# A four-head conv and retention trunk in fp32: Strassen over all 16 K tiles, sample dot products on ScalarE, and pairs that overlap

## The chip, the core and the metric

One core of one Trainium2 chip runs the whole program. The metric is the device time of one execution in microseconds; the median over runs is compared. The kernel has five engines to spread its work over: TensorE (PE in the profile, its weight loads PEld), VectorE (DVE), ScalarE (ACT), GpSimd (POOL) and SyncE (SP), which here only issues DMAs.

## The reference

Two layers (DEPTH = 2) of a hybrid decoder are run for a prompt of 512 positions and for 8 samples of one new position each; the kernel treats them as one matrix of T = 520 columns. Everything is fp32. The core of one layer:

```python
h = rmsnorm(x, norm_g)
z = h @ w_in                      # 2048 -> 8192
b_c, c_c, x_c, g_c, q, k, v, g_r = split_projection(z)
conv_y, new_buf = short_conv(c_c * x_c, conv_buf, conv_w)
y_conv = b_c * conv_y * jax.nn.silu(g_c)
q = rope(q.reshape(Bsz, L, RET_HEADS, RET_HEAD_DIM), pos)
k = rope(k.reshape(Bsz, L, RET_HEADS, RET_HEAD_DIM), pos) * (RET_HEAD_DIM ** -0.5)
...
o, new_S = retention(q, k, v, ret_S.astype(jnp.float32), retention_log_gamma())
...
x = x + jnp.concatenate([y_conv, y_ret], axis=-1) @ w_out
x = x + jax.nn.sigmoid(x @ w_pg) * (p_i @ w_ple)
```

Retention has 4 heads of 256. For a sample there is only one position, so a head's step is a rank-one update of its 256 x 256 state with k and v, and then the product of q with the new state: 256 dot products. The states and the last conv inputs are outputs too.

## The kernel before

**Tiles and pairs.** D = 2048 is 16 K tiles of 128. Every big product (w_in, w_out, w_pg) goes by *pairs*: two blocks of 128 output rows, each 520 columns wide in two halves of 260 (LEFT and RIGHT). A product in fp32 is three fp32r matmuls (`mm3`, L247 to L249): weight high part by operand high and low part, weight low part by operand high part. High and low parts of the weights are made on the core by `split_w`: ScalarE copies the rounded high part (L229), VectorE subtracts it for the low part (L230). They lie in a ring of 60 tiles of 128 columns (SPLIT), the raw weights in one of 32 (RAW).

**Strassen.** `pair` computes two output blocks either with `plain` (64 tile products) or with `strassen` over the first s K tiles, in Winograd's form: seven products of s/2 tiles instead of eight, with four sums of weight blocks on VectorE (`add`, L319) and sums of the operands' halves (`operand_sums`, L413 to L416), which are made once and shared by all pairs. The other 16 - s tiles are added in the ordinary way. With s < 16 four PSUM banks hold the sums (a, b, c, d), with s = 16 three do. ScalarE copies banks to slots or to other banks (`copy`), VectorE adds them up (`plus`); both are recorded at L307. Five banks (`Banks`) serve these products.

**Which s a pair has.** The tables HEADS, CONVS, OUT_ROWS and GATES name s for each pair. Before, the pairs of the heads are at 14 (after 0 and 8 at the start of layer 0, 0 at the start of layer 1), and the conv pairs at 14, 14, then 13 times 16, then 14.

**Stages of a layer.** Heads: for each of 4 heads four pairs (q, k, v, gate), `rope` and `silu` on VectorE and ScalarE, and the chunked retention of the prompt in nine steps taken up between pairs (`later`, `aside`). Conv: 16 pairs, with a short convolution on VectorE. Then 8 output pairs and 8 gate pairs (the last pair of the last layer is taken apart).

**Sample steps.** `sample_step` is called between and within pairs of heads and convs, 32 times a layer. It loads one state (`st`, 128 x 512) and one row of q and k on all partitions (`kb`), decays the state on ScalarE (L776), adds k times v on VectorE in two halves (L780), sends the state out from GpSimd's queue (L781), and takes the dot products with q on VectorE, each half with one multiply-and-sum instruction (L784), which the chip runs as the main instruction and a read of the accumulator. `osum` collects them until `sample_norm` at the end of the convs.

**What sets the order.** The code issues instructions in program order with priorities (`tc.high_priority`, with WPRIO for the weights' splits and sums), and a scheduler then orders each engine's queue with a simulated timeline. Each engine runs its queue in order; semaphores join them. SP issues the weight loads.

Of the kernel before, what the change touches and what calls it, by code (L numbers as in the profile page):

```python
# [9 lines left out]
AF = mybir.ActivationFunctionType  # L10
# [3 lines left out]
P = 128  # L14
D = 2048
KT = D // P
DEPTH = 2
SEQ = 512
NS = 8
# [32 lines left out]

HEADS = [[0, 0, 0, 8] + [14] * 12, [0] + [14] * 15]
CONVS = [[14] * 2 + [16] * 13 + [14]] * 2
OUT_ROWS = [[0, 8, 16, 16, 16, 16, 16, 0]] * 2
# [136 lines left out]
def trunk_kernel(  # L192
# [69 lines left out]
    def acc(n):  # L262
        return [banks.get() for _ in range(n)]
# [25 lines left out]

    def strassen(x, src0, src1, s, step=None):  # L290

# [3 lines left out]
        ops = x.ops  # L295
        x.supply(min(s + CH, KT))
        assert len(x.sums) >= q
        k1, k2 = at(ops, range(0, s, 2), LEFT), range(1, s, 2)
        t1, t2, t3, t4 = ([t[i] for t in x.sums[:q]] for i in range(4))
        step = step or (lambda n: None)  # L300
        a, b, d = acc(3)
        c = banks.get() if s < KT else None
        z0, z1 = get(), get()

        def early(fn, *args):
# [29 lines left out]

        w11 = raws(src0, 0)
        times(a, w11, k1, True, False)
        step(1)
        copy(d, a)
        w21, w22 = raws(src1, 0), raws(src1, q)  # L340
# [14 lines left out]
        if c is None:  # L355
            copy(z0[:, LEFT], d)
        aside()
        times(a, w11, t3, False, True)
        raw_ring.put(w11)
        step(5)  # L360
        if c is None:
            plus(z1[:, RIGHT], a, z1[:, RIGHT])
        else:
            copy(z1[:, LEFT], a)
        while middle:
            middle.pop(0)()
        times(b, w21, at(ops, k2, RIGHT), False, True)
        raw_ring.put(w21)
        step(6)
        if c is None:  # L370
            plus(z0[:, RIGHT], b, z0[:, RIGHT])
        times(a, w22, t4, False, True)
# [12 lines left out]
        if c is not None:  # L385
            plus(z1[:, RIGHT], c, z1[:, LEFT])
            copy(z0[:, LEFT], d)
            plus(z0[:, RIGHT], b, z0[:, RIGHT])
            banks.put(c)
        copy(z1[:, LEFT], a)  # L390
        banks.put(d, b, a)
        step(8)
# [3 lines left out]
    def pair(x, src, m, n, nxt=None):  # L396
# [4 lines left out]
        if s:  # L401
            z = strassen(x, src[m], src[m + 1], s, (lambda i: x.free(i, nxt)) if last else None)
        else:
            z = plain(x, src[m], src[m + 1], (lambda a, b: x.free_tiles(a, b, nxt)) if last else None)
# [18 lines left out]
    class Operands:  # L423


        def __init__(self, rows, load, reserve=0, whole=False, gain=None):
            self.rows, self.load, self.reserve, self.whole, self.gain = rows, load, reserve, whole, gain
            self.sent = []
            self.ops = [None] * KT
            self.sums = []  # L430
            self.ready = 0
            first = max(rows[0], min(FIRST, max(rows))) // 2
# [283 lines left out]
    for l in range(DEPTH):  # L716
# [57 lines left out]
        def sample_step(h, b, st, kb):  # L774

            keep(S.activation(st[:, :512], st[:, :512], AF.Identity, scale=gam(h)))  # L776
            k = kb[:, 256:512]
            for e in range(2):
                c = slice(256 * e, 256 * e + 256)
                keep(V.scalar_tensor_tensor(st[:, c], k, vs[:, h, e, b : b + 1], st[:, c], MUL, ADD))  # L780
            SIDE.dma_start(o_rets[l, h, b], st[:, :512])  # L781
            for e in range(2):
                c = slice(256 * e, 256 * e + 256)
                V.tensor_tensor_reduce(k, st[:, c], kb[:, :256], 1.0, 0.0, MUL, ADD, osum[:, e, h, b : b + 1])  # L784
            put(st, kb)
# [31 lines left out]
        def retain(h):  # L817
# [10 lines left out]
            for d in range(2):  # L828
                S.activation(qks[:, d, :NS], q[d][:, SEQ:T], AF.Copy)
            aside_copy(h, 0, q)  # L830
# [6 lines left out]
            for d in range(2):  # L837
                S.activation(qks[:, 2 + d, :NS], kf[d][:, SEQ:T], AF.Copy)
            aside_copy(h, 2, kf)
# [639 lines left out]
```

## Time and profile before

| | |
|---|---|
| median of 3 runs | 2169.55 us (2167.43 to 2171.86) |
| the profiled execution's span | 2167.3 us |
| between its span and the runs' median | 2.25 us |
| PE busy | 2147.8 us, 99%, 17861 matmuls |
| DVE busy | 1896.1 us, 87% |
| ACT busy | 1264.5 us, 58% |
| POOL busy | 430.6 us, 20% |
| DMA | 387.31 MB, mean 179 GB/s |

A row of a group of instructions has the line, the engine, the operation, what is written and read with shapes, the count, then the busy time in us and the mean of one in ns, and last the idle time of the engine just before them and what ended it. A row of waits has who waited for whom, the us in total, how often, and the longest. A row of windows has the stretch, its length, then busy time and count of PE, PEld, DVE, ACT and POOL, the granted clock of TensorE, and the DMA's share and rate. Matmuls overlap each other, so 282 ns for one is its length in the pipeline, and not the distance from one to the next.

### The profile page before, as it was taken

To read this page: it belongs to the slowest core of one execution; us is meant where nothing else is said; L and a number is where in the kernel's file an instruction comes from. 1 tells how busy PE (TensorE), PEld (TensorE's weight loads), DVE (VectorE), ACT (ScalarE), POOL (GpSimd) and SP (SyncE) were. 2 spreads that over 40 slices of the span, in tenths; PEclk is the share of its full clock that TensorE was granted. 3 is DMA by queue.
4 is the path that set the end of the run, shared out by engine and by line. 5 is a ranking of instruction groups with operands and counts; after the bars stand their busy time and mean duration, and the time that the engine had idled before them with its cause. 6 is when DMAs were issued, how large, how long until landed. Compare 5 with 4: busy or idle time off the path is not lost. (4 is left out here: it accounts for less than half of the span.)

```text
span 2167.3 us, 48178 instructions
## 1 busy us (share of the span) xinstructions
PE 2147.8 (99%) x17861; PEld 2142.1 (99%) x17861; DVE 1896.1 (87%) x3849; ACT 1264.5 (58%) x2647; POOL 430.6 (20%) x746
## 2 busy tenths in 40 slices
PE   9999999999999999999999999999999999999998
PEld 9999999999999999999999999999999999999998
DVE  8889988998999987987997988989999998879884
ACT  8656655565555655655765655565645555456565
POOL 2313222211001211200212222231111022011011
PEclk9999999999999999999999999999999999999999
DMA  8555565545543745645645566664464355566455
GB/s 288 171 175 197 181 217 184 178 157 175 158 129 118 238 156 187 215 154 160 215 144 175 172 213 191 189 209 170 151 182 149 120 158 202 176 207 200 128 164 198
DMA packets 182861, 387.31 MB, mean 179 GB/s; under 512 B 25888, under 2 KB 56352, under 8 KB 182624
## 3 DMA queue, kind: packets, MB, share of 16 engines
q1 hardware_dynamic: 128704, 212.98, 31.6%
q0 software_dynamic: 53056, 169.84, 23.8%
q8 instruction: 140, 2.29, 0.4%
q10 hardware_dynamic: 864, 1.39, 0.2%
q14 instruction: 97, 0.79, 0.1%
HBM read 318.96 MB, written 65.15 MB: 177 GB/s over the span
## 5 line engine op out<-in xcount | busy, mean ns | idle before, releaser
L247 PE MATMUL ps_g<-slot,split 128*128 128x260 f32 x5465 | 1531.6, 284 | 7.2 <-ACT slot L307 2.9
L248 PE MATMUL ps_g<-slot,split 128*128 128x260 f32 x5465 | 1534.3, 282 | 0.3 <-DVE slot L555 0.3
L249 PE MATMUL ps_g<-slot,split 128*128 128x260 f32 x5461 | 1519.9, 283 | 0.5 <-DVE split L230 0.5
L229 ACT ACTIVATE split<-raw 128x512 fp32r<-128x512 f32 (+2 forms) x1347 | 777.3, 596 | 583.1 <-DVE raw L319 213.2
L247 PEld LDWEIGHTS ps_g<-slot,split 128*128 128x128 f32 x5465 | 1024.0, 188 | 10.1 <-ACT slot L307 3.7
L248 PEld LDWEIGHTS ps_g<-slot,split 128*128 128x128 f32 x5465 | 1028.5, 188 | 0.5 <-DVE slot L555 0.5
L249 PEld LDWEIGHTS ps_g<-slot,split 128*128 128x128 f32 x5461 | 1019.8, 188 | 1.0 <-DVE split L230 1.0
L230 DVE TENSOR_TENSOR split<-raw,split 128x512 fp32r<-128x512 f32 (+2 forms) x1346 | 849.2, 652 | 172.5 <-PE ps_g L248 85.4
L319 DVE TENSOR_TENSOR raw<-raw 128x512 f32<-128x512 f32 (+1 forms) x660 | 428.9, 660 | 32.5 <-DMA raw<-wi 23.7
L307 ACT ACTIVATE slot<-ps_g 128x260 f32<-128x260 f32 x336 | 127.4, 381 | 140.6 <-PE ps_g L249 122.7
L551 ACT ACTIVATE slot<-slot 128x520 fp32r<-128x520 f32 (+1 forms) x212 | 109.2, 562 | 46.6 <-DVE slot L414 11.1
L552 DVE TENSOR_TENSOR slot<-slot,slot 128x520 fp32r<-128x520 f32 (+1 forms) x212 | 124.4, 620 | 4.1 <-ACT slot L551 3.9
L781 POOL DMA_DIRECT2D o_rets<-slot x64 | 35.3, 552 | 351.6 <-DVE slot L780 131.7
L307 DVE TENSOR_TENSOR slot<-ps_g,slot 128x260 f32<-128x260 f32 x168 | 70.9, 424 | 6.0 <-PE ps_g L249 3.7
L869 POOL DMA_DIRECT2D slot<-hs x64 | 46.2, 724 | 118.7 <-DVE split L230 42.7
L814 POOL DMA_DIRECT2D hs<-slot x64 | 35.6, 556 | 139.3 <-DVE slot L755 61.3
L780 DVE SCALAR_TENSOR_TENSOR slot<-slot,vs,slot 128x256 f32<-128x256 f32 x128 | 56.1, 481 | 4.5 <-ACT slot L776 4.3
L746 DVE TENSOR_TENSOR slot<-slot,slot 128x520 f32<-128x520 f32 x80 | 55.8, 698 | 4.7 <-DMA o_rets<-slot 3.7
L770 POOL DMA_DIRECT2D slot<-sret x64 | 35.5, 554 | 114.6 <-ACT split L229 37.3
L1058 POOL DMA_DIRECT2D slot<-x1s x76 | 40.8, 538 | 87.6 <-PE ps_g L249 27.2
L1209 POOL DMA_DIRECT2D x2s<-slot x30 | 16.4, 545 | 201.6 <-DVE slot L1204 200.6
L771 POOL DMA_DIRECT2D slot<-kq x64 | 34.9, 547 | 106.0 <-DVE slot L876 22.2
(217 smaller groups left out, 1733.8 us busy)
## 6 DMA issues: line engine op xcount, KB each, us to landing
raw<-wi SPq DMA_DIRECT2D x377, 256.0 KB, 3.9
raw<-wo SPq DMA_DIRECT2D x128, 256.0 KB, 5.4
raw<-wg SPq DMA_DIRECT2D x122, 256.0 KB, 4.1
raw<-wi SPq DMA_DIRECT2D x136, 192.0 KB, 4.0
slot<-x1s POOLq DMA_DIRECT2D x76, 260.0 KB, 5.1
slot<-sret POOLq DMA_DIRECT2D x64, 256.0 KB, 4.0
hs<-slot POOLq DMA_DIRECT2D x64, 256.0 KB, 4.0
slot<-hs POOLq DMA_DIRECT2D x64, 256.0 KB, 5.2
```

The costliest lines, as they stand in the source:

```text
L229: S.activation(hi, raw, AF.Copy)
L230: V.tensor_tensor(lo, raw, F(hi), SUB)
L247: PE.matmul(out, wh, xh, start=start, stop=False, skip_group_check=more)
L248: PE.matmul(out, wh, xl, start=False, stop=False, skip_group_check=more)
L249: PE.matmul(out, wl, xh, start=False, stop=stop, skip_group_check=more)
L307: fn(*args)
L319: V.tensor_tensor(out[:, n], x[:, n], y[:, n], op)
L551: keep(S.activation(hi, src[:, n], AF.Copy))
L552: V.tensor_tensor(lo, src[:, n], F(hi), SUB)
L746: V.tensor_tensor(out[:, n], v, table[:, n], MUL)
L780: keep(V.scalar_tensor_tensor(st[:, c], k, vs[:, h, e, b : b + 1], st[:, c], MUL, ADD))
L869: SIDE.dma_start(t[:, :512].rearrange("p (m n) -> p m n", m=2), src)
```

## The change

Four edits.

1. The tables: 12 + 15 head pairs go from 14 to 16 tiles, and the first two conv pairs of each layer too. Only the last conv pair of a layer stays at 14.
2. `strassen` with s = 16 takes its sixth product (b) ahead of the fifth (a), and gives banks back as soon as they are read: d after its copy, b after its sum.
3. If the next pair has 16 tiles as well, the first product of that pair and the copy of it (`begin`) are issued ahead of this pair's last product, and handed over in `x.begun`. This holds for heads, convs, output and gate pairs.
4. `sample_step`: one product on VectorE of the whole state (512 columns) with q, which is read twice by a broadcast; then ScalarE sums each half with an ACTIVATE Copy whose accumulator goes to `osum`. For that, k and q change places in `qks` and `kb`.

```diff
-HEADS = [[0, 0, 0, 8] + [14] * 12, [0] + [14] * 15]
-CONVS = [[14] * 2 + [16] * 13 + [14]] * 2
+HEADS = [[0, 0, 0, 8] + [16] * 12, [0] + [16] * 15]
+CONVS = [[16] * 15 + [14]] * 2
...
-    def strassen(x, src0, src1, s, step=None):
+    def strassen(x, src0, src1, s, step=None, ahead=None):
...
-        a, b, d = acc(3)
-        c = banks.get() if s < KT else None
-        z0, z1 = get(), get()
...
-        w11 = raws(src0, 0)
-        times(a, w11, k1, True, False)
+        def begin(src):
+            a, d = acc(2)
+            w = raws(src, 0)
+            times(a, w, k1, True, False)
+            copy(d, a)
+            return a, d, w
+
+        a, d, w11 = x.begun or begin(src0)
+        x.begun = None
+        b = banks.get()
+        c = None if whole else banks.get()
+        z0, z1 = get(), get()
         step(1)
-        copy(d, a)
...
         if c is None:
             copy(z0[:, LEFT], d)
+            banks.put(d)
         aside()
+        if whole:
+            times(b, w21, at(ops, k2, RIGHT), False, True)
+            raw_ring.put(w21)
+            step(6)
+            plus(z0[:, RIGHT], b, z0[:, RIGHT])
+            banks.put(b)
         times(a, w11, t3, False, True)
...
-        times(b, w21, at(ops, k2, RIGHT), False, True)
-        raw_ring.put(w21)
-        step(6)
-        if c is None:
-            plus(z0[:, RIGHT], b, z0[:, RIGHT])
+        if not whole:
+            times(b, w21, at(ops, k2, RIGHT), False, True)
+            raw_ring.put(w21)
+            step(6)
+        elif ahead is not None and len(banks.free) > 1 and all(ops[0:KT:2]):
+            x.begun = begin(ahead)
         times(a, w22, t4, False, True)
...
-            z = strassen(x, src[m], src[m + 1], s, (lambda i: x.free(i, nxt)) if last else None)
+            z = strassen(x, src[m], src[m + 1], s, (lambda i: x.free(i, nxt)) if last else None,
+                         src[m + 2] if s == KT and x.rows[n + 1 : n + 2] == [KT] else None)
...
-            k = kb[:, 256:512]
+            k, q = kb[:, :256], kb[:, 256:512]
...
+            both = kb[:, :512].rearrange("p (e d) -> p e d", e=2)
+            V.tensor_tensor(both, st[:, :512].rearrange("p (e d) -> p e d", e=2), q.unsqueeze(1).broadcast_to([P, 2, 256]), MUL)
             for e in range(2):
-                c = slice(256 * e, 256 * e + 256)
-                V.tensor_tensor_reduce(k, st[:, c], kb[:, :256], 1.0, 0.0, MUL, ADD, osum[:, e, h, b : b + 1])
+                S.activation(both[:, e], both[:, e], AF.Copy, accum_out=osum[:, e, h, b : b + 1])
```

What the scheduler makes of it is seen in the engines' orders. First, ScalarE where one pair passes into the next in the heads of layer 0, before. `ps_g_3624` is the first bank (a) of the next pair, `ps_g_3626` its d, and `ps_g_3308` the bank a of this pair, whose last eviction is the last row; `split` are weights' high parts, and `ps_o` belongs to the retention.

```order
L229 ACTIVATE split_73<-raw_72 128x512 x2
L307 ACTIVATE ps_g_3626<-ps_g_3624 128x260
L229 ACTIVATE split_73<-raw_72 128x384
L988 ACTIVATE slot10_247_3475<-ps_o_3452,shift_3465,rstp_3464 128x256 x2
...
L229 ACTIVATE split_73<-raw_72 128x512
L307 ACTIVATE slot54_243_3313<-ps_g_3308 128x260
```

The same place with the change, where `ps_g_4691` is the next pair's a, `ps_g_4692` its d, and `ps_g_4387` this pair's a (`ps_kt` is of the retention).

```order
L935 ACTIVATE slot57_302_4616<-ps_kt_4611,vec_74 128x256
L229 ACTIVATE split_73<-raw_72 128x512 x4
L304 ACTIVATE ps_g_4692<-ps_g_4691 128x260
L229 ACTIVATE split_73<-raw_72 128x512
L304 ACTIVATE slot27_298_4490<-ps_g_4387 128x260
```

In both, the copy of the next pair's first product stands ahead of this pair's last eviction; what moved is that now all splits are 512 wide.

Second, a sample step on VectorE in the heads of layer 0, before: `slot65_238_3286` is the state, `slot3_239_3287` holds q and k.

```order
L780 SCALAR_TENSOR_TENSOR slot65_238_3286<-slot3_239_3287,vs_81,slot65_238_3286 128x256 x2
L230 TENSOR_TENSOR split_73<-raw_72,split_73 128x512
L230 TENSOR_TENSOR split_73<-raw_72,split_73 128x384
L230 TENSOR_TENSOR split_73<-raw_72,split_73 128x512
L784 ISA slot3_239_3287,osum_82<-slot65_238_3286,slot3_239_3287 128x256
L784 ISA osum_82 128x1
```

With the change, VectorE at a step of layer 0's heads (`slot61_277_4190` the state, `slot3_278_4191` k and q), and after it ScalarE around the sums of the same step.

```order
L797 SCALAR_TENSOR_TENSOR slot61_277_4190<-slot3_278_4191,vs_81,slot61_277_4190 128x256 x2
L230 TENSOR_TENSOR split_73<-raw_72,split_73 128x512
L800 TENSOR_TENSOR slot3_278_4191<-slot61_277_4190,slot3_278_4191 128x512
L230 TENSOR_TENSOR split_73<-raw_72,split_73 128x512
L304 TENSOR_TENSOR slot60_281_4207<-ps_g_4206,slot60_281_4207 128x260
```

```order
L847 ACTIVATE qks_3908<-slot64_276_3912 128x8
L229 ACTIVATE split_73<-raw_72 128x512 x4
L802 ACTIVATE slot3_278_4191,osum_82<-slot3_278_4191 128x256 x2
L229 ACTIVATE split_73<-raw_72 128x512
L304 ACTIVATE ps_g_4388<-ps_g_4387 128x260
L229 ACTIVATE split_73<-raw_72 128x512
```

The two sums with their reads have left VectorE's queue, one product has come, and the sums now stand in ScalarE's queue among the splits and evictions.

More of the change, by code (lines that the diff above doesn't have):

```diff
@@ L296, in strassen @@
         x.supply(min(s + CH, KT))
+        whole = s == KT
         assert len(x.sums) >= q
@@ L360, in strassen @@
         step(5)
-        if c is None:
+        if whole:
             plus(z1[:, RIGHT], a, z1[:, RIGHT])
@@ L366, in strassen @@
             middle.pop(0)()
-        times(b, w21, at(ops, k2, RIGHT), False, True)
-        raw_ring.put(w21)
-        step(6)
-        if c is None:
-            plus(z0[:, RIGHT], b, z0[:, RIGHT])
+        if not whole:
[4 more added lines that the diff above has]
+            x.begun = begin(ahead)
         times(a, w22, t4, False, True)
@@ L389, in strassen @@
             banks.put(c)
+            banks.put(d, b)
         copy(z1[:, LEFT], a)
-        banks.put(d, b, a)
+        banks.put(a)
         step(8)
@@ L430, in __init__ @@
             self.sums = []
+            self.begun = None
             self.ready = 0
@@ L828, in retain @@
             for d in range(2):
-                S.activation(qks[:, d, :NS], q[d][:, SEQ:T], AF.Copy)
+                S.activation(qks[:, 2 + d, :NS], q[d][:, SEQ:T], AF.Copy)
             aside_copy(h, 0, q)
@@ L837, in retain @@
             for d in range(2):
-                S.activation(qks[:, 2 + d, :NS], kf[d][:, SEQ:T], AF.Copy)
+                S.activation(qks[:, d, :NS], kf[d][:, SEQ:T], AF.Copy)
             aside_copy(h, 2, kf)
```

## The prediction

> **What bounds the kernel now.** I read the page first: busy time of each engine, and the rows over the span for TensorE and its clock.
>
> ```profile
> span 2167.3 us, 48178 instructions
> PE 2147.8 (99%) x17861; PEld 2142.1 (99%) x17861; DVE 1896.1 (87%) x3849; ACT 1264.5 (58%) x2647; POOL 430.6 (20%) x746
> PE   9999999999999999999999999999999999999998
> PEclk9999999999999999999999999999999999999999
> ```
>
> TensorE is busy all the way at the full granted clock. The span is 2167.3 us and the runs' median 2169.55, so 2.25 us lie around the span. I make the sum on the span and add them back.
>
> Next came the waits of TensorE. A busy PE could still be a PE that is fed late, so what it waited for decides.
>
> ```profile
> PE ps_g L247 <- ACT slot L307: 2.9, 4, 1.3
> PE ps_g L247 <- ACT ps_g L307: 1.6, 2, 1.2
> PE ps_g L247 <- ACT split L229: 1.5, 2, 1.3
> PE ps_vt L913 <- DMA slot<-hs: 0.9, 1, 0.9
> PE ps_g L249 <- DVE split L230: 0.5, 1, 0.5
> ```
>
> These are total, times and longest. In 2167 us TensorE lost under 10 us to other engines, 6.0 us of it before a product's first matmul (L247) for an eviction or a split.
>
> Third, the windows, to see where VectorE stands in the stages that the change touches. The first is one plain stretch in the heads; the second answer has the heads of layer 0, its conv pairs of 16 tiles, and the same two stages of layer 1.
>
> ```profile
> 200.00:250.00 50.00, 50.00 (x420) 50.00 (x419) 47.05 (x101) 30.28 (x67) 10.12 (x17) 1.00 0.60 184
> ```
>
> ```profile
> core 0: us, PE busy (x) PEld busy (x) DVE busy (x) ACT busy (x) POOL busy (x), PEclk, DMA share, GB/s
> 101.00:400.00 299.00, 299.00 (x2501) 298.93 (x2500) 269.80 (x600) 179.43 (x397) 79.94 (x139) 1.00 0.60 191
> 424.00:664.00 240.00, 239.06 (x1997) 238.88 (x1996) 221.23 (x436) 134.61 (x272) 29.43 (x50) 1.00 0.49 151
> 1144.00:1464.00 320.00, 319.79 (x2675) 319.50 (x2675) 283.68 (x629) 189.48 (x419) 82.47 (x140) 1.00 0.61 191
> 1488.00:1700.00 212.00, 211.76 (x1768) 211.35 (x1767) 192.67 (x378) 118.54 (x242) 28.95 (x49) 1.00 0.51 158
> ```
>
> In the heads 420 matmuls pass in 50 us, one per 0.119 us, with VectorE at 94% in that stretch and 90.2% over the whole of layer 0's heads. So a matmul taken away is worth 0.119 us as long as VectorE keeps up, and VectorE is the engine to watch.
>
> **The change, part by part.**
>
> *Fewer matmuls.* A pair of s tiles by Strassen has 7 products of s/2 tiles, and the other 16 - s tiles cost 4 tile products each; a tile product is 3 matmuls. At 14 that is 49 + 8 = 57, at 16 it is 56: 3 matmuls less for each pair. The number of pairs: HEADS has 12 + 15 rows that go from 14 to 16, CONVS 2 in each layer, 31 in all (the last conv pair stays at 14). The built order agrees: it has 93 matmuls less. 93 x 0.119 = 11.1 us off TensorE, all on the path that sets the end.
>
> The Trainium skill, "TensorE: Matmul & The Clock Gate", section "Wait — 56ns, not 53.3ns?", puts a warm matmul's start to start at N / 2.4 GHz plus about 2.5 ns. For 260 columns that would be 110.8 ns and 10.3 us, an estimate from that page; this trace has 119 ns, and the measurement decides.
>
> *The weights' work on VectorE and ScalarE.* The rows by shape:
>
> ```profile
> L230 DVE TENSOR_TENSOR split<-raw,split 128x512 fp32r<-128x512 f32 x1031 | 695.0, 690 | 147.8 <-PE ps_g L248 81.2 <-ACT split L229 51.8 <-issue 6.1
> L229 ACT ACTIVATE split<-raw 128x512 fp32r<-128x512 f32 x1032 | 632.3, 626 | 462.3 <-DVE raw L319 188.2 <-PE ps_g L249 166.4 <-PE ps_g L248 45.1
> L319 DVE TENSOR_TENSOR raw<-raw 128x512 f32<-128x512 f32 x520 | 354.1, 688 | 17.6 <-DMA raw<-wi 12.1 <-DMA raw<-wo 2.9
> L230 DVE TENSOR_TENSOR split<-raw,split 128x384 fp32r<-128x384 f32 x249 | 137.1, 555 | 16.2 <-ACT split L229 9.9 <-PE ps_g L248 3.4 <-ACT slot L551 1.9
> L229 ACT ACTIVATE split<-raw 128x384 fp32r<-128x384 f32 x249 | 127.2, 518 | 84.0 <-DVE raw L319 25.0 <-PE ps_g L248 24.2 <-PE ps_g L249 17.9
> L319 DVE TENSOR_TENSOR raw<-raw 128x384 f32<-128x384 f32 x140 | 77.4, 554 | 14.9 <-DMA raw<-wi 11.6 <-DMA raw<-wg 2.8
> L230 DVE TENSOR_TENSOR split<-raw,split 128x256 fp32r<-128x256 f32 x66 | 27.3, 423 | 8.5 <-ACT split L229 7.6 <-PE ps_g L248 0.8
> L229 ACT ACTIVATE split<-raw 128x256 fp32r<-128x256 f32 x66 | 27.3, 415 | 36.7 <-DMA raw<-wi 29.0 <-PE ps_g L248 5.2 <-PE ps_g L249 1.9
> L307 ACT ACTIVATE ps_g<-ps_g 128x260 f32<-128x260 f32 x121 | 45.1, 373 | 16.4 <-PE ps_g L249 16.1
> ```
>
> A pair of 14 splits 7 x (512 + 384) columns and twice 256; a pair of 16 splits 14 x 512. VectorE: 14 x 0.690 = 9.66 us instead of 7 x (0.690 + 0.555) + 2 x 0.423 = 9.56. Its four weight sums: 8 x 0.688 = 5.50 instead of 4 x (0.688 + 0.554) = 4.97. Together +0.635 us a pair, +19.7 us in 31 pairs. ScalarE: splits 8.76 instead of 8.84, and one copy from bank to bank less (0.373): -0.45 us a pair, -13.9 us. SyncE has two weight loads less a pair, of the same bytes. None of this is on the path while TensorE is fed.
>
> *The dot products.* Each of the 64 sample steps had two multiply-and-sum instructions on VectorE, each with a read of the accumulator. Now it has one 512-wide product there and two summing copies on ScalarE.
>
> ```profile
> L784 DVE CUSTOM_DVE_ANT_0 slot<-slot,slot 128x256 f32<-128x256 f32 x128 | 53.9, 421 | 0.0
> L784 DVE DVE_READ_ACCUMULATOR2_ANT osum<- 128x1 f32 x128 | 11.1, 87 | 0.0
> ```
>
> VectorE: 2 x (0.421 + 0.087) = 1.016 goes, one product at the 0.688 of a 512-wide sum comes: -0.328 us a step, -21.0 us in 64. The net on VectorE over the kernel is -1.3 us. ScalarE's summing form does not stand in the trace: I take 0.415, the 256-wide copy, since the work is the same, and 0.415 + 0.087 as the other end if its accumulator is read out as VectorE's is. That is 53 to 64 us, so ScalarE's net is +39 to +50 us on 1264.5, about 61% of the new span. On the path I take 0. What hides it is the lead of the split weights.
>
> ```profile
> ACT split L229 <- PE ps_g L248: 21.9, 32, 2.3
> ACT split L229 <- PE ps_g L249: 18.8, 33, 1.8
> ```
>
> In 101 to 400 us ScalarE stood 65 times until TensorE had freed a piece of the split ring, that is, with the ring full. The new sums wait for VectorE's product, and behind them in ScalarE's queue stand splits and evictions, for which VectorE and TensorE wait; a full ring of 60 tiles, at 8 high and 8 low tiles and 24 matmuls a product, is 3.75 x 24 x 0.119 = 10.7 us of cover. Without any cover 64 x 0.83 = 53 us would show.
>
> The Trainium skill, "ScalarE: Activation LUTs", section "Rules for kernel authors", says to give add and multiply to VectorE, not ScalarE, which speaks against this edit. In this trace the 256-wide copy on ScalarE (0.415) costs no more than the 256-wide product and sum on VectorE (0.421 and 0.087), and ScalarE is the idler engine.
>
> *Pairs run into each other.* The next pair's first product and its copy are now emitted ahead of this pair's last product. But in the order before, ScalarE's copy of the next pair's first product already stood ahead of this pair's last eviction: the scheduler had done this. So I take 0. The ends are -6.0 us (all three L247 waits above go) and +6.0 us (as many new ones). The sum of the last pair of operands in layer 0 is now due at the third pair; it stands 8 splits later in the new order, so its end is 8 x 0.69 = 5.5 us of loss, and I take 0, as it is due only at the end of that pair's second product.
>
> *VectorE in the heads, where the room is least.* Pairs and steps in the windows of layer 0, heads first, then convs:
>
> ```profile
> L319 DVE TENSOR_TENSOR raw<-raw 128x512 f32<-128x512 f32 (+1 forms) x102 | 62.1, 620 | 1.3 <-DMA raw<-wi 0.9
> L784 DVE CUSTOM_DVE_ANT_0 slot<-slot,slot 128x256 f32<-128x256 f32 x39 | 16.4, 422 | 0.0
> ```
>
> ```profile
> L319 DVE TENSOR_TENSOR raw<-raw 128x512 f32<-128x512 f32 x91 | 61.9, 689 | 2.4 <-DMA raw<-wi 2.1
> ```
>
> 102 sums at 8 a pair are 12.75 pairs, and 39 sums are 19.5 steps. VectorE goes from 269.8 to 269.8 + 12.75 x 0.635 - 19.5 x 0.328 = 271.5 us, TensorE from 299 to 299 - 12.75 x 0.357 = 294.4: 92.2%. The conv pairs of 16 now have 221.23 of 240, 92.2% as well, and TensorE was busy 239.06 of them. So the load that the heads get is one that the kernel already carries. Layer 1 has more room (283.68 of 320 now).
>
> The sum: 2167.3 - 11.1 = 2156.2 us of span, plus 2.25 around it: 2158.5 us.
>
> **The rivals.**
>
> *Slower: VectorE's gaps are latency, not room.* In 101 to 400 us VectorE idles 299 - 269.8 = 29.2 us, 2.29 a pair. If it needs all of these, its chain takes 271.5 + 29.2 = 300.7 us against TensorE's 294.4: 0.49 us a pair, 13.3 us in the 27 head pairs, and the gain of 11.1 turns into a loss of 2.2. The sums in ScalarE's queue add to it: VectorE now waits 69.3 us for splits, by these rows,
>
> ```profile
> L229 ACT ACTIVATE split<-raw 128x512 fp32r<-128x512 f32 (+2 forms) x1347 | 777.3, 596 | 583.1 <-DVE raw L319 213.2 <-PE ps_g L249 186.2 <-DMA raw<-wi 75.6
> L230 DVE TENSOR_TENSOR split<-raw,split 128x512 fp32r<-128x512 f32 (+2 forms) x1346 | 849.2, 652 | 172.5 <-PE ps_g L248 85.4 <-ACT split L229 69.3 <-issue 6.4
> ```
>
> 0.089 us for each us of ScalarE's splits, so 39 us more are 3.5 us more. 2169.55 + 2.2 + 3.5 = 2175 us. It decides once VectorE cannot give up 6.3 of its 29.2 us. For it: few of these gaps are a full ring. Against it: the conv pairs (91 / 8 = 11.4) get by with (240 - 221.23) / 11.4 = 1.65 us a pair, and 271.5 + 12.75 x 1.65 = 292.5 is still under 294.4. Chance 0.07.
>
> *No change: the new order brings as many waits as it saves.* VectorE's order is new from end to end, and the waits of TensorE are chance meetings. A late operand pair at the start (5.5 us) and a second set of L247 waits (6.0) would leave 2169.55 - 11.1 + 11.5 = 2170 us; half of that is still in my own range. For it: TensorE waits where one stage passes into the next, as here between 704 and 1124 us, and these places are reordered too.
>
> ```profile
> PE ps_g L247 <- ACT split L229: 1.3, 1, 1.3
> PE ps_g L247 <- ACT slot L307: 0.8, 1, 0.8
> ```
>
> Against: there are under 10 us of them in the whole span. Chance 0.10.
>
> *More: the seams close.* The 6.0 us of L247 waits go as well: 2152.5 us. For it: that edit is aimed at just these. Against: the scheduler crossed the seams already. Chance 0.10.
>
> *The overlap edit does nothing* is part of my forecast, as worked out above; the other two edits show in the order.
>
> **How the numbers follow.** The forecast, TensorE-bound as now, has 0.73. A measurement of this kernel tells about 0.2% (4.3 us), so faster means under 2165.2 and slower over 2173.9. The forecast and the closed seams are faster: 0.83. No change 0.10, slower 0.07. The range goes from the closed seams, 2152, to 2166, the forecast with three quarters of the new waits (8 us); it leaves out the rest of the no-change case and the slower one.
>
> **What would show it.** Right: 93 matmuls less (17768), 420 in 50 us in the heads, VectorE near 92% there, no L784 kind on VectorE, 128 sums on ScalarE of 0.41 to 0.50 us, L247's waits still under 10 us. Wrong: in the heads' windows TensorE busy well under the window's length, with waits for splits (the slower rival), or several waits of over 1 us at seams (the no-change rival).

## The result, and the profile after

The changed kernel took 2216.41 us (median of 4 runs, 2212.48 to 2217.06), the kernel before 2169.03 us beside it (2167.43 to 2171.86): a ratio of 1.0215, 95% interval 1.0200 to 1.0229. It is 47 us slower, where 11 us less were forecast. In e19 and e20 below, one execution each took 5260.54 and 4214.6 us; these two are not counted in the times given for them.

The page of the kernel after, its span and engine rows:

```profile
span 2214.5 us, 47612 instructions
PE 2156.5 (97%) x17768; PEld 2139.0 (97%) x17768; DVE 1908.2 (86%) x3595; ACT 1302.7 (59%) x2810; POOL 444.7 (20%) x746
```

The 93 matmuls are gone (17768), yet the span is 47.2 us longer. TensorE's idle time rose from 2167.3 - 2147.8 = 19.5 us to 2214.5 - 2156.5 = 58.0 us, 38.5 us more. Its busy time rose by 8.7 us, although 93 x 0.119 = 11.1 us of matmuls left it: busy time hides the first tenths of a microsecond of each gap, because a matmul's modelled end lies behind the next one's start, and it grows where the clock drops. Counted from start to start over all matmuls of the trace (what goes beyond 0.119 us, where that is over 0.15 us; called gaps from here on), TensorE lost 15.4 us before and 64.4 us after. The mean granted clock went from 0.999 to 0.996, which is 0.003 x 2214.5 = 6.6 us. Together -11.1 + 49.0 + 6.6 = 44.5 of the 47.2 us.

The longest waits of TensorE after (total, times, longest):

```profile
PE ps_g L247 <- ACT split L229: 11.4, 7, 4.9
PE ps_g L249 <- DVE split L230: 8.8, 16, 1.5
PE ps_g L247 <- ACT slot L304: 8.2, 11, 1.7
PE ps_g L247 <- ACT slot L568: 5.9, 4, 2.2
PE ps_g L247 <- DVE slot L304: 5.0, 9, 1.5
PE ps_g L247 <- ACT ps_g L304: 4.9, 3, 2.9
```

Before, the first of these was 1.5 us and the whole list 11.2; now the whole list is 49.8. It isn't one wait: splits that come late (from both engines) and evictions that come late, some sixty of 0.2 to 4.9 us. The groups on the page after show the same from the other side:

```profile
L247 PE MATMUL ps_g<-slot,split 128*128 128x260 f32 x5434 | 1531.0, 285 | 38.5 <-ACT split L229 11.4
L229 ACT ACTIVATE split<-raw 128x512 fp32r<-128x512 f32 (+1 forms) x1285 | 775.1, 623 | 575.8 <-DVE raw L316 229.1
L230 DVE TENSOR_TENSOR split<-raw,split 128x512 fp32r<-128x512 f32 x1284 | 847.9, 680 | 145.1 <-ACT split L229 73.9
L316 DVE TENSOR_TENSOR raw<-raw 128x512 f32<-128x512 f32 (+1 forms) x660 | 443.7, 680 | 88.6 <-DMA raw<-wg 42.9
```

ScalarE's splits now wait 229.1 us for VectorE's sums of weights (213.2 before, L319 there), and these sums wait 88.6 us, 42.9 of it for loads of wg, where before they waited 32.5 and 2.8. VectorE's splits wait less for TensorE to free the ring (48.6 us for L248's matmuls, 85.4 before): it is full less often.

Where it happens, by the four stretches of the prediction's table (heads, convs, heads, convs):

```profile
core 0: us, PE busy (x) PEld busy (x) DVE busy (x) ACT busy (x) POOL busy (x), PEclk, DMA share, GB/s
101.00:400.00 299.00, 290.35 (x2383) 287.16 (x2383) 265.73 (x501) 181.88 (x417) 79.90 (x137) 0.99 0.58 185
424.00:664.00 240.00, 237.78 (x1983) 237.37 (x1982) 222.79 (x408) 145.42 (x316) 34.63 (x53) 1.00 0.52 160
1144.00:1464.00 320.00, 301.46 (x2459) 297.10 (x2458) 273.15 (x504) 180.75 (x409) 76.97 (x134) 0.99 0.55 173
1488.00:1700.00 212.00, 209.87 (x1753) 209.22 (x1753) 195.99 (x364) 129.72 (x292) 39.63 (x61) 1.00 0.55 168
```

The conv pairs still keep TensorE busy for nearly all of it with VectorE at 222.79 / 240 = 92.8%. The heads do not, with VectorE at 88.9% in layer 0 and 85.4% in layer 1: 118 and 216 matmuls fewer pass there than before. Set against the time that the passed matmuls need, VectorE's load is much the same in both: 265.73 of 2383 x 0.119 = 283.6 us in the heads (93.7%), 222.79 of 236.0 us in the convs (94.4%). VectorE's busy share does not tell a stage that is fed from one that isn't.

These stretches are fixed in time, so in a slower kernel they hold other work: a stretch can have shifted by up to 45 us against before, and before, the heads of layer 0 end at 374 us. Cut instead where TensorE's product matmuls reach the number that each stage's pairs need, the heads of both layers took 769.5 us against 738.3 before, though 81 matmuls (9.6 us) are gone there; the convs 685.1 against 687.7, the output pairs 348.5 against 340.4, the gate pairs 406.3 against 395.7. So 31 of the 47 us lie in the heads, 11 in the gates and 8 in the output pairs.

The longest stall, from the timeline of after (start, length, instruction, idle time before it and its releaser):

```profile
1254.06 0.68 DVE L800 TENSOR_TENSOR slot<-slot,slot 128x512 f32<-128x512 f32 x1
1254.66 0.87 DVE L1016 SCALAR_TENSOR_TENSOR slot<-ps_ot,vec,slot 128x256 f32<-128x256 f32 x2
1255.45 0.68 DVE L316 TENSOR_TENSOR raw<-raw 128x512 f32<-128x512 f32 x1
1257.17 0.63 ACT L229 ACTIVATE split<-raw 128x512 fp32r<-128x512 f32 x1 [1.49 <-DMA raw<-wi]
1257.85 0.59 PE L247 MATMUL ps_g<-slot,split 128*128 128x260 f32 x1 [4.87 <-ACT split L229]
1258.23 0.42 PE L248 MATMUL ps_g<-slot,split 128*128 128x260 f32 x1
1258.45 0.42 PE L247 MATMUL ps_g<-slot,split 128*128 128x260 f32 x1
1258.67 0.42 PE L248 MATMUL ps_g<-slot,split 128*128 128x260 f32 x1
```

A product's first split comes 4.87 us late, because its load came late. SyncE had held that load back until VectorE's split of another block gave its place in the raw ring free, at 1253.5 us. SyncE's waits from 1244 to 1260 us have, as total, times and longest,

```profile
SPq L309 <- DVE split L230: 6.2, 3, 5.2
```

so this load waited for VectorE. Behind the stall the matmuls start 0.22 us apart, not 0.119. The windows of 5 us around it (the third figure from the end is the granted clock):

```profile
1250.00:1255.00 5.00, 2.98 (x26) 2.77 (x24) 4.79 (x9) 3.06 (x7) 0.59 (x1) 1.00 0.42 149
1255.00:1260.00 5.00, 2.15 (x10) 2.15 (x11) 3.87 (x8) 1.96 (x8) 0.73 (x1) 0.56 0.33 101
1260.00:1265.00 5.00, 5.00 (x34) 5.00 (x34) 2.46 (x6) 1.61 (x5) 1.46 (x3) 0.76 0.26 107
1265.00:1270.00 5.00, 5.00 (x44) 5.00 (x43) 3.37 (x7) 2.20 (x5) 2.65 (x6) 1.00 0.26 76
```

The clock is down to 0.56 and 0.76 for two windows, so the stall is paid a second time in part: by the timeline the matmuls stay 0.22 us apart until 1262.35 us, 4.5 us from the stall's end, which is some 20 matmuls or 2 us lost. The Trainium skill, "TensorE: Matmul & The Clock Gate", section "What's actually happening", says that the clock falls to half after an idle window of about 3.4 us and is released after as much sustained work; the 4.87 us of idle time and the 4.5 us at 0.22 us here are in line with it, and no run here measures the 3.4 us themselves.

### The profile page after: what moved, and what is told of

Read it like the earlier page. It is cut to its first block, busy times and chain, and to the rows that moved or that the text cites. A ratio compares the mean times of both kernels' runs of the same rounds, so it can differ in the third digit from the quotient of the medians.

```text
span 2214.5 us, 47612 instructions
## 1 busy us (share of the span) xinstructions
PE 2156.5 (97%) x17768; PEld 2139.0 (97%) x17768; DVE 1908.2 (86%) x3595; ACT 1302.7 (59%) x2810; POOL 444.7 (20%) x746
## 4 chain that ended last, share of the span: by engine, by line
PE 61%; issue 13%; DVE 11%; DMA 10%; ACT 3%; POOL 2%; SPq 0%; DVEq 0%; POOLq 0%; ACTq 0%
PE ps_g L247 19%; PE ps_g L249 19%; PE ps_g L248 19%; DMA raw<-wi 5%; DVE split L230 4%; DVE raw L316 2%; ACT split L229 1%; DMA raw<-wg 1%; DVE slot L569 1%; DMA slot<-x2s 1%; DMA slot<-ys 1%; ACT slot L568 1%; DMA hs<-slot 1%; DVE slot L797 0%; POOL slot L1076 0%
## 5 line engine op out<-in xcount | busy, mean ns | idle before, releaser
L247 PE MATMUL ps_g<-slot,split 128*128 128x260 f32 x5434 | 1531.0, 285 | 38.5 <-ACT split L229 11.4
L248 PE MATMUL ps_g<-slot,split 128*128 128x260 f32 x5434 | 1528.5, 283 | 0.3 <-DVE slot L572 0.3
L229 ACT ACTIVATE split<-raw 128x512 fp32r<-128x512 f32 (+1 forms) x1285 | 775.1, 623 | 575.8 <-DVE raw L316 229.1
L248 PEld LDWEIGHTS ps_g<-slot,split 128*128 128x128 f32 x5434 | 1024.2, 189 | 0.9 <-DVE slot L572 0.5
L230 DVE TENSOR_TENSOR split<-raw,split 128x512 fp32r<-128x512 f32 x1284 | 847.9, 680 | 145.1 <-ACT split L229 73.9
L316 DVE TENSOR_TENSOR raw<-raw 128x512 f32<-128x512 f32 (+1 forms) x660 | 443.7, 680 | 88.6 <-DMA raw<-wg 42.9
L802 ACT ACTIVATE slot<-slot 128x256 f32<-128x256 f32 x128 | 51.9, 407 | 18.7 <-DVE slot L800 17.6
```

What stands on the lines that cost most here:

```text
L229: S.activation(hi, raw, AF.Copy)
L230: V.tensor_tensor(lo, raw, F(hi), SUB)
L247: PE.matmul(out, wh, xh, start=start, stop=False, skip_group_check=more)
L248: PE.matmul(out, wh, xl, start=False, stop=False, skip_group_check=more)
L316: V.tensor_tensor(out[:, n], x[:, n], y[:, n], op)
L802: S.activation(both[:, e], both[:, e], AF.Copy, accum_out=osum[:, e, h, b : b + 1])
```

## The theories, and the experiments

- **Theory 1, lost cover.** Next pair's first product used to lie between the last product's loads and their use; run ahead, it is used up. **1b** adds that the loads now come into other places of the raw ring, which come free later.
- **Theory 2, VectorE.** Pairs of 16 in the heads give VectorE work for which its gaps there have no room.
- **Theory 3, ScalarE's sums** hold up splits and evictions in its queue.
- **Theory 4, the order.** The queues are static and planned before the run; any edit has them planned anew, and the order before happened to wait least.

### The three edits one by one

e1, the tables alone, e2, the dot products alone, and e3, the pair's new order alone (the heads stay at 14, so that it acts on the pairs of 16 in the gates, the output and the convs):

```
# e1_tables, against before
-HEADS = [[0, 0, 0, 8] + [14] * 12, [0] + [14] * 15]
-CONVS = [[14] * 2 + [16] * 13 + [14]] * 2
+HEADS = [[0, 0, 0, 8] + [16] * 12, [0] + [16] * 15]
+CONVS = [[16] * 15 + [14]] * 2
# e2_dots, against before
-                V.tensor_tensor_reduce(k, st[:, c], kb[:, :256], 1.0, 0.0, MUL, ADD, osum[:, e, h, b : b + 1])
+            V.tensor_tensor(both, st[:, :512].rearrange("p (e d) -> p e d", e=2), q.unsqueeze(1).broadcast_to([P, 2, 256]), MUL)
...
+                S.activation(both[:, e], both[:, e], AF.Copy, accum_out=osum[:, e, h, b : b + 1])
# e3_overlap, against the whole change: the edits in strassen kept, the others undone
-HEADS = [[0, 0, 0, 8] + [16] * 12, [0] + [16] * 15]
-CONVS = [[16] * 15 + [14]] * 2
+HEADS = [[0, 0, 0, 8] + [14] * 12, [0] + [14] * 15]
+CONVS = [[14] * 2 + [16] * 13 + [14]] * 2
...
```

> Only the tables are changed: 31 pairs go from 14 to 16 K tiles; overlap and dot products as before. Theory 1 (the overlap of pairs is the cause: the next pair's first product, run ahead, takes away the work that covered the next weights' load): the 93 matmuls are gained, 2158 to 2161 us, and the heads wait as little as before. Theory 2 (VectorE's and ScalarE's chain can't feed pairs of 16 in the heads): most of the loss is here, 2190 to 2215 us, with TensorE waiting for splits in the heads only.

> Only the dot products are moved: one product on VectorE, two sums on ScalarE; pairs and overlap as before. Theories 1 and 2 both expect no change, 2167 to 2172 us. Theory 3 (the sums in ScalarE's queue, 0.407 plus 0.188 us for each half, hold up splits and evictions): slower, 2180 us or more, with TensorE waiting for ScalarE in the heads and convs.

> Only strassen is changed: sixth product ahead of the fifth, banks given back early, next pair's first product ahead of this one's last; head pairs stay at 14, so the overlap acts in conv, output and gate pairs alone. Theory 1: slower in the output and gate stages by the 10 to 12 us that they lose with the whole change, 2178 to 2183 us, nothing in the heads. Theory 2: no change, 2167 to 2172 us.

Measured: e1 2180.5 us (ratio 1.0059, 1.0044 to 1.0074), e2 2174.19 (1.0030, 1.0017 to 1.0043), e3 2184.79 (1.0081, 1.0064 to 1.0098). None gains, and each loses something; the three losses, 12.8, 6.5 and 17 us or so, come to some 36 of 47 us. e1 and e2 fell between the expectations, e3 came out just above theory 1's. Gaps of TensorE: 33.3, 19.8 and 28.7 us, where before has 15.4. The tables lose although 11.1 us of matmuls are gone with them.

### Is any order made anew as bad?

Two controls change nothing of the work: e10 gives the raw ring 40 tiles and the split ring 56, e11 one more slot. Both have the queues planned anew. e11 is the cleaner one, since it only adds room; e10 also takes four tiles from the split ring.

```
# e10_before_ring40, against before
-RAW = 32
+RAW = 40
...
-SPLIT = 60
+SPLIT = 56
# e11_before_slot76, against before
-NSLOT = 75
+NSLOT = 76
```

> The kernel before with the raw ring of 40 and the split ring of 56, a control. Both theories: 2164 to 2172 us, since it waits hardly at all; were it faster by more than 5 us, the gain of the other two would be that of the ring and not of the cause.

> The kernel before with one buffer slot more (76 instead of 75): the same work with more room, but the scheduler lays the queues out anew. Theory 4 (every rebuilt order loses, since the order before happens to wait least): 2173 to 2185 us. Theories 1 and 2: no change, 2164 to 2171 us.

Measured: e10 2180.8 us (1.0055, 1.0038 to 1.0072), e11 2183.65 (1.0067, 1.0052 to 1.0082), with gaps of 27.8 and 25.0 us. Theories 1 and 2 had expected no loss; theory 4 had e11 right. So the same work in another order cost 12 to 15 us in both, and the order before looks like an unusually good one. That is the size of each single edit's loss, so e2 and e3 show nothing beyond theory 4 by their times alone. e1 is as slow as these controls with 11 us less to do.

### The tables and the whole, in other orders

The same two changes of size on the tables and on the whole change, and the pairs of edits (the diffs are those above, put together):

```
# e4_tables_dots = e1 and e2          # e15_tables_overlap = e1 and e3
# e7_all_ring40 = the whole, e10      # e8_tables_ring40 = e1, e10
# e12_all_slot76 = the whole, e11     # e17_tables_slot76 = e1, e11
```

> Tables and dot products, without the overlap. Theory 1: 2158 to 2161 us, the gain that was forecast. Theory 2: 2190 to 2210 us. Theory 3: slower than the tables alone by 10 us or more.

> Tables and overlap, dot products as before on VectorE. If the loss where tables and overlap meet doesn't need the sums on ScalarE: 2205 to 2222 us. If the sums are part of it: 2185 to 2198 us, the tables' 2180 plus the overlap's 17 at most.

> The whole change, with a raw ring of 40 tiles instead of 32 (five places for a pair's four weight blocks) and, to make room, a split ring of 56 instead of 60. Theory 1b (a weight block can be loaded only into the place of a block that is still to be split, and the overlap takes away the product that covered the load): the gate pairs' waits of 1 to 2 us go and most of those in the heads, 2165 to 2185 us. Theory 2 (VectorE's load in the heads): the gate pairs gain about 10 us, the heads nothing, 2200 to 2208 us.

> The tables alone, with the raw ring of 40 and the split ring of 56. Theory 1b: the waits that pairs of 16 brought into the heads (18 us) go, 2158 to 2166 us. Theory 2: as with the tables alone, 2176 to 2184 us.

> The whole change with one buffer slot more: again the same work in another order. Theory 4: the size of the loss moves by more than 8 us, up or down. Theories 1 and 2 (the loss lies in the change itself): 2210 to 2222 us.

> The tables alone with one buffer slot more, so in another order. Against the kernel before with the same 76 slots (2183.7 us) the 93 matmuls less are worth 11 us if pairs of 16 bring no waits of their own: 2168 to 2176 us. If pairs of 16 in the heads wait in any order: 2180 to 2195 us.

Measured, with TensorE's busy time in the heads' two stretches (101 to 400 and 1144 to 1464 us, 619 us together):

| kernel | heads | us | ratio, 95% interval | TensorE busy of 619 us |
|---|---|---|---|---|
| before | 14 | 2169.03 | | 618.79 |
| e10, e11 | 14 | 2180.8, 2183.65 | (above) | 616.97, 612.81 |
| e2, e3 | 14 | 2174.19, 2184.79 | (above) | 614.59, 616.47 |
| e1 | 16 | 2180.5 | 1.0059 (1.0044 to 1.0074) | 602.00 |
| e4 | 16 | 2181.34 | 1.0063 (1.0048 to 1.0078) | 605.12 |
| e17 | 16 | 2200.24 | 1.0146 (1.0128 to 1.0165) | 597.86 |
| e8 | 16 | 2207.58 | 1.0180 (1.0165 to 1.0195) | 596.02 |
| e7 | 16 | 2184.69 | 1.0074 (1.0059 to 1.0089) | 605.02 |
| e15 | 16 | 2213.25 | 1.0208 (1.0192 to 1.0223) | 592.62 |
| e12 | 16 | 2213.49 | 1.0197 (1.0173 to 1.0221) | 601.40 |
| after | 16 | 2216.41 | 1.0215 (1.0200 to 1.0229) | 591.81 |

Two rows of that kind as the trace gives them, the sums over both stretches for e11 (14 tiles, the worst of its kind here):

```profile
sum 619.00, PE 612.81 PEld 610.55 DVE 544.44 ACT 361.08 POOL 165.55; mean PE 306.40 PEld 305.28 DVE 272.22 ACT 180.54 POOL 82.78
```

and for e4 (16 tiles, the best of its kind):

```profile
sum 619.00, PE 605.12 PEld 600.11 DVE 555.88 ACT 378.34 POOL 167.13; mean PE 302.56 PEld 300.05 DVE 277.94 ACT 189.17 POOL 83.56
```

The two groups don't meet: with all of the work done, heads of 14 keep TensorE busy for 612.8 us or more, heads of 16 for 605.1 or less. The four kernels of the section on the overlap fall in with their groups: e9, with heads of 14, has 617.90, and e16, e18 and e19, with heads of 16, have 591.38, 600.49 and 600.61. That is not chance of the order alone; pairs of 16 in the heads starve TensorE. How much, the order decides: the tables' four orders without the new pair (e1, e4, e17, e8) span 27 us for the same matmuls. It doesn't decide all: e12, the whole in another order, stayed at 2213.49, as theories 1 and 2 had expected and theory 4 had not. e8 and e17 came out slower than any of their expectations.

Theory 3 falls as the cause of the large loss: e15 has the dot products on VectorE as before and is as slow as the whole change (2213.25), and e4 with them is as e1 without. Theory 1b as first meant falls too: a fifth place in the raw ring takes 32 us off the whole (e7), but adds 27 us to the tables (e8) and 13 to the kernel before.

### Less work for VectorE

If VectorE is what the heads run out of, they are fed again once it has less to do. These kernels leave out the arithmetic of the 64 sample steps (state and query are still loaded, the state is stored as it came, the sums are zero), so part of the output isn't computed. e13 has the tables, e14 the whole change, e20 the kernel before.

```
# e13, e20 against e1 and before (e14 drops the same steps in its form)
-            keep(S.activation(st[:, :512], st[:, :512], AF.Identity, scale=gam(h)))
...
-                keep(V.scalar_tensor_tensor(st[:, c], k, vs[:, h, e, b : b + 1], st[:, c], MUL, ADD))
...
-                V.tensor_tensor_reduce(k, st[:, c], kb[:, :256], 1.0, 0.0, MUL, ADD, osum[:, e, h, b : b + 1])
```

> The tables alone, with the arithmetic of the sample steps left out (decay, rank-one update and dot products; the loaded state is sent out as it is, the sums are zero): VectorE has 127 us less to do and ScalarE 46 us. Theory 2 (VectorE's load in the heads is why pairs of 16 wait): 2156 to 2162 us, with under 8 us of waits in heads and convs. If the load is not the cause, 2172 to 2182 us.

> The whole change with the arithmetic of the sample steps left out: VectorE has 100 us less, ScalarE 122 us. Theory 2: the heads' waits go and the gate stages' stay, 2165 to 2175 us. Theory 1b (places of the raw ring and lost cover, whatever VectorE's load): 2195 to 2215 us.

> The kernel before with the arithmetic of the 64 sample steps left out (state and query are loaded and the state stored as it is, the sums are zero): the control for the tables without that arithmetic, which took 2165.4 us. TensorE does as many matmuls as before. If VectorE's load is what the pairs of 16 in the heads suffer from, then without that load the tables' 93 matmuls should show in full: this control at about 2176 us, 11 us over the tables' 2165. If leaving the steps out only makes a luckier order, the control is itself well under 2176, at 2160 to 2168.

Measured: e13 2165.42 us (0.9989, 0.9979 to 0.9998), e14 2186.47 (1.0085, 1.0067 to 1.0104), e20 2184.53 (1.0075, 1.0055 to 1.0096). The tables, which lose in every order with the full work, now take 19.1 us less than their control: the 11.1 us of the matmuls and 8.0 more. e13 came out 3 us above what theory 2 had expected and e14 between the two expectations. The sums over the heads of e13:

```profile
sum 619.00, PE 610.03 PEld 608.79 DVE 523.73 ACT 343.69 POOL 172.90; mean PE 305.02 PEld 304.39 DVE 261.86 ACT 171.85 POOL 86.45
```

610.0 us for the pairs of 16 (6.0 of the missing 9 are one wait for an eviction elsewhere, ps_ot), 608.1 in e14, and 607.9 for the pairs of 14 in e20: with VectorE 36 us lighter in these stretches than in e1 (559.90), 14 and 16 are fed alike. In e13 VectorE's splits stood 44.0 us with the ring full there (21.5 and 22.5), in e1 11.9 us (5.0 and 6.9): it has a lead again. By the stages' matmul counts, all twenty kernels fall into four groups in the heads (us, both layers):

| heads | kernels | gaps of TensorE | its waits for splits |
|---|---|---|---|
| 14 | before, e2, e3, e9, e10, e11 | 4.3 to 9.8 | 0.0 to 3.5 |
| 16 | e1, e4, e7, e8, e12, e15 to e19, after | 21.9 to 38.1 | 5.7 to 19.2 |
| 16, no arithmetic of the sample steps | e13, e14 | 14.1, 17.0 | 0.4, 0.0 |
| 14, no arithmetic of the sample steps | e20 | 15.0 | 0.0 |

This is theory 2 for the waits for splits: they come with the pairs of 16 in all eleven kernels and are gone without the arithmetic of the sample steps. It isn't the whole of the heads' loss. What TensorE still waits for in the heads of e13, e14 and e20 are nearly all evictions (11.0, 14.8 and 11.3 us), and e20 has three before ps_ot (7.1 us) that the kernel before doesn't have, so that it loses in the heads although it has less to do. No theory here explains these, other than a new order. A second reservation: the steps left out also relieve ScalarE, by 352.78 - 343.69 = 9 us here. The control came out at 2184.53 where 2176 was the slower of its expectations, and the 19.1 us are not far beyond what an order is worth, so only their sign is read.

### The overlap: gates, heads, sixth product

e9 is e3 without the begin ahead in the gate pairs; e18 is e7 without it; e16 is the whole change without it in the heads; e19 is the whole with the sixth product back behind the fifth.

```
# e9, e18: no begin ahead in the gate pairs (e16: the same with a flag set for the heads)
-                         src[m + 2] if s == KT and x.rows[n + 1 : n + 2] == [KT] else None)
+                         src[m + 2] if s == KT and x.rows[n + 1 : n + 2] == [KT] and not x.gate else None)
# e19: moved behind the fifth product
+        times(b, w21, at(ops, k2, RIGHT), False, True)
+        raw_ring.put(w21)
+        step(6)
+        if whole:
+            plus(z0[:, RIGHT], b, z0[:, RIGHT])
+            banks.put(b)
```

> The overlap alone as in e3_overlap, but gate pairs don't start the next pair's first product ahead. Theory 1b: in a gate pair the second weight block of the next pair (w22) loads into the place of this pair's last one, and the first product of the next pair was the work that covered it; with it back in its place the waits of the gate stages (about 10 us) go, 2172 to 2178 us. Were these waits a chance of the new order, it would stay at 2182 to 2188 us.

> The whole change with raw ring 40 and split ring 56, and gate pairs that don't start the next product ahead. With five places the gate pairs had few waits left (about 3 us), so the lost-cover theory expects little: 2178 to 2187 us. If the gate stages lose for another reason, 2170 to 2177 us.

> The whole change, but head pairs don't start the next pair's first product ahead; conv, output and gate pairs do. If the meeting of overlap and pairs of 16 in the heads is what costs 30 us: 2185 to 2198 us, with the heads' waits down to those of the tables and dot products without overlap. If it is anything else of the change: 2208 us or more.

> The whole change with the sixth product put back behind the fifth; the pairs still begin the next one ahead. Tables alone took 2180.5 us, tables and the overlap 2213, the whole 2216, and without the begin ahead in the heads it stayed at 2219. If the sixth product ahead of the fifth brings the extra 33 us, this kernel falls to 2180 to 2190 us. If they come from how the pairs of 16 happen to fall in an order made anew, it can land anywhere from 2180 to 2216; 2205 or more would clear the sixth product's place.

Measured: e9 2177.74 us (1.0040, 1.0025 to 1.0055), e18 2189.64 (1.0104, 1.0079 to 1.0129), e16 2218.9 (1.0226, 1.0211 to 1.0242), e19 2193.56 (1.0126, 1.0109 to 1.0143).

In layer 0's gate stage (900 to 1100 us) VectorE's waits of e3 read

```profile
DVE raw L316 <- DMA raw<-wg: 21.0, 11, 2.9
DVE split L230 <- PE ps_g L248: 0.8, 1, 0.8
```

and those of e9

```profile
DVE split L230 <- PE ps_g L248: 16.6, 21, 1.3
DVE raw L316 <- DMA raw<-wg: 0.3, 1, 0.3
```

With the next pair begun ahead VectorE stands before the loads and has no lead; without it stands before a full ring, and the loads are there. e9 is 7 us faster than e3. The raw ring explains it: by the code, in a gate pair the last block of weights (w22) of the next pair goes into the place of this pair's last block, before as after. Before, two products lay between that place's release and its use; with one of them run ahead, 24 x 0.119 = 2.9 us are left to cover a load, a sum and a split. The swap of VectorE's wait is theory 1 shown at this place, and so is its price: of the 7 us by which e9 is faster, the gate stages have all (399.8 us by matmul count, in e3 407.2). The seven kernels that begin ahead in the gate pairs with a raw ring of 32 (e3, e12, e14, e15, e16, e19, after) take 404.4 to 408.3 us there, the thirteen others 394.7 to 400.0. Among these is e7, which begins ahead with a ring of 40 (399.1), so with one place more there is nothing left to win (e18 against e7).

In the heads the begin ahead is not the cause: e16 does without and is as slow as the whole. e18 was 3 us slower than its slower expectation. e19 came out between its two, 23 us better than the whole and 13 worse than e1, and so decides nothing: it is within the 27 us that the tables' orders span.

## Why the prediction was wrong

*Fewer matmuls:* right in count; 93 are gone. At 0.119 us each they are 11.1 us, but no kernel that does all of the work got them as a gain; e13 against e20, where TensorE waits for hardly any split, has the sign.

*The weights' work, and the dot products:* mis-sized, both in the same direction. VectorE's rows on the pages of e1 and of e2:

```profile
PE 2143.5 (98%) x17768; PEld 2134.2 (98%) x17768; DVE 1919.8 (88%) x3787; ACT 1258.8 (58%) x2554; POOL 432.8 (20%) x746
```

```profile
PE 2147.8 (99%) x17861; PEld 2142.0 (99%) x17861; DVE 1893.5 (87%) x3657; ACT 1316.7 (61%) x2903; POOL 435.6 (20%) x746
```

Against 1896.1 the tables add 23.7 us (forecast 19.7) and the dot products take away 2.6 us (forecast 21.0); both together, e4, add 18.2, where the net was put at -1.3. What failed here was to add up durations. The timeline of before shows why:

```profile
103.08 0.69 DVE L230 TENSOR_TENSOR split<-raw,split 128x512 fp32r<-128x512 f32 x1
103.68 0.42 DVE L307 TENSOR_TENSOR slot<-ps_g,slot 128x260 f32<-128x260 f32 x1
104.02 0.56 DVE L230 TENSOR_TENSOR split<-raw,split 128x384 fp32r<-128x384 f32 x1
104.48 0.42 DVE L784 CUSTOM_DVE_ANT_0 slot<-slot,slot 128x256 f32<-128x256 f32 x1
104.83 0.09 DVE L784 DVE_READ_ACCUMULATOR2_ANT osum<- 128x1 f32 x1
104.83 0.70 DVE L746 TENSOR_TENSOR slot<-slot,slot 128x520 f32<-128x520 f32 x1
```

Each instruction starts 0.07 to 0.10 us ahead of the end of the one before, and the accumulator's read takes no time of its own: it starts together with the next instruction. From start to start, a 512-wide one costs 0.60 us, a 384-wide one 0.46, a 260-wide one 0.34, a product with its read 0.35; over the whole trace, where the next one follows at once, the medians are 0.602, 0.469, 0.338 and 0.343. By these, a sample step gives up 2 x 0.343 and takes 0.602, a gain of 0.08 us and not 0.328, and a pair gets 22 x 0.602 - 11 x (0.602 + 0.469) - 2 x 0.338 = +0.79 us and not +0.635 (the 256-wide splits counted as 260). That makes 24.5 us for the tables' 31 pairs, where 23.7 were measured, and -5.4 us for the 64 steps, where -2.6 were. For layer 0's heads it is 269.8 + 12.75 x 0.79 - 19.5 x 0.08 = 278.3 us of 294.4, 94.5% and not 92.2%.

*"So the load that the heads get is one that the kernel already carries":* this is the step that decided, and it failed. It took a busy share, measured in the conv pairs, as proof that the heads would be fed too. The shares did come out alike (93.7% and 94.4% of the time that the matmuls need), and still the convs are fed and the heads starve: TensorE's gaps in the heads went from 4.3 us to 38.0. What differs is not settled in full: between the splits of the heads stand rope and retention steps on VectorE (the stall above has 0.87 us of L1016 in it), in the convs those of the short convolution, but no run here separates them.

*The slower rival* had, for the waits for splits, the right mechanism (VectorE's gaps are latency, not room), a chance of only 0.07 and a price too low. Its sign came, TensorE busy well under the heads' stretches with waits for splits. With the start-to-start costs it gives (278.3 + 29.2 - 294.4) / 12.75 = 1.03 us a pair, 28 us in 27 pairs, and -11.1 + 28 = +17 on 2169.55, 2186 us; the four orders of the tables without the new pair gave 2180.5 to 2207.6. The evictions that came late are not in it.

*"On the path I take 0" for ScalarE's sums:* held within the size of an order (e4, e15). The sums added 1316.7 - 1264.5 = 52.2 us to ScalarE (53 to 64 forecast); what failed of that step was only the relief of VectorE.

*Pairs run into each other, 0 with ends of 6 us:* too small. The begin ahead cost 7 us in the gate pairs alone (e9 against e3), a place that the prediction did not look at; it looked at the seams' evictions, and not at the loads whose cover the first product was.

*The no-change rival* held the second large error: new waits were allowed 11.5 us because the order before had under 10 (11.2 by the whole list). That few waits are an exception was to be had only from a control: the same work in a new order lost 12 to 15 us (e10, e11).

*What stays open:* the whole change is 36 us slower than the tables alone in e1. By the stages' matmul counts 21 of these lie in the heads (769.5 and 748.4 us), 10 in the gates, where they are the begin ahead, and 6 in the output pairs, where no group of kernels stands clearly apart. In the heads the whole change, e15 and e16 take 767.7 to 769.5 us, the tables without the new pair 747.5 to 760.8. Neither the dot products (e15) nor the begin ahead in the heads (e16) make that difference; the sixth product's new place may (e19, 754.8), or the plan's order may: e12, the whole change with a slot more, takes 759.2 there. No run tells these apart. No version that does all of the work was faster than the kernel before.

## What to carry to other kernels

Add up an engine's work from start to start in the timeline, not from durations, and count an accumulator's read at what it adds there. Where queues are planned ahead and the order now waits for almost nothing, an edit may lose that luck, so run the old work in a new order as a control before a single edit's loss or gain is believed. A product that is run ahead was somebody's cover: look for the load whose landing it hid.

## What the runs showed of the hardware

The summing copy on ScalarE is two instructions there, by its line in the trace of after (min, median, max ns):

```profile
L802 ACT ACTIVATE slot<-slot x128: 397/403/421, 110.8 to 1769.9; 128x256 f32<-128x256 f32 x128
L802 ACT ACTIVATION_READ_ACCUMULATOR slot<-slot x128: 184/187/203, 111.1 to 1770.2; 128x1 f32 x128
```

By durations that is 0.59 us a sum and 76 us in all; ScalarE's busy time grew by 52.2 us in e2, 0.41 us a sum, so the read lies almost wholly beside its neighbours. And a stall of 4.87 us cost TensorE more than itself: the granted clock stood at 0.56 and 0.76 in the two windows of 5 us from its last part on, which came to some 2 us more.
